# A token mixer's shift and scale from a four-column stationary operand, with a buffer for each weight tile, and other places for a gate chain and two gate sums

## The chip, the core and the metric

The kernel runs on one core of a Trainium2 chip. Its engines are TensorE (PE in the rows; PEld is its weight load), VectorE (DVE), ScalarE (ACT), GpSimd (POOL) and SyncE (SP), which issues the loads and stores. The metric is the time of one execution on the device in microseconds.

## What is computed

One layer of a bidirectional mLSTM mixer with a ConvGLU channel mixer, on 1024 latent tokens and 256 context tokens of width 1024. Each sub-layer is normalised and then shifted and scaled by a conditioning vector:

```python
mod = silu(c) @ w_mod + b_mod                      # w_mod (1024, 6 * 1024)
sh1, sc1, ga1, sh2, sc2, ga2 = split(mod, 6)
csh1, csc1, ... = split(silu(c_ctx) @ w_mod + b_mod, 6)
hc = rmsnorm(ctx, g_mix) * (1 + csc1) + csh1
hx = rmsnorm(x, g_mix) * (1 + sc1) + sh1
y  = mlstm_mixer(hx, hc, ...)                      # 4 heads, 2 directions, input and forget gates
x  = x + ga1 * y
hx = rmsnorm(x, g_ffn) * (1 + sc2) + sh2
gate, val = split(hx @ w_up, 2)                    # width 2816 each
x  = x + ga2 * ((silu(conv3(gate) + b_conv) * val) @ w_down)
return rmsnorm(x, g_final)
```

## The kernel before

Nearly all products are made from fp32 operands that `split` (L76) cuts in two: ScalarE casts a high part (`S.copy`), VectorE subtracts it for a low part, both in fp32r. `mm3` (L85) then makes three matmuls, high by high (L86), low by high (L87) and high by low (L88). The parts lie in eight buffers of the tag `w`. The writer's order is a wish: the framework places the instructions of each engine, and an engine runs its own in the order in which they then stand.

**The prelude.** `crow` holds `c` and `c_ctx`; after a transpose and a Silu they are `sct` (128 x 8 x 2: row block k, and the two vectors w), with the parts `sch` and `scl`. The loop at L211 goes over the eight row blocks k of `w_mod`, and in each over the two column blocks (shift, scale). It loads a tile `mr` of 128 x 1024 into one of six buffers and multiplies its two halves into four accumulators `mps` (2 rows by 512). For k = 1, 3, 5 the tile is split and goes through `mm3`; for the others it is multiplied in fp32 as it is (L227). Small loads stand between the tiles, and at k = 6 the context tokens are loaded and normalised (`x_load(0)`, `x_norm(0)`). Then come the first value weights `wv0` (loaded and split at L232), the latent tokens, and the way from accumulator to coefficient: `mrow` (copied out of PSUM), `mt` (sixteen transposes), `mts` (plus the bias), `smod` in `vec` (scale by gain). `x_trans` (L175) transposes the tokens and applies them (`xf`, L187), and the projections follow (`proj_v`, `pv`).

**The gate chain.** `gate_rows` (L393) makes from the gates' pre-activations `gt` all that the scans need: log-sigmoid, running sums and maxima along the tokens on VectorE, then `xc`, four columns of ends, transposed by TensorE as `cp`; a scan over the chunks in `gs`; `bp`, `mp` and `op` back through TensorE; `mx` is stored to `mdram`, and `cco`, `bco` are the coefficients. After it stands the projection of keys and queries of head 0, `proj_qk(0)`: `pk_256`, `pk_768`, `pk_0` (the context tokens, 24 matmuls of 256 columns) and `pq_256`, `pq_768`. The framework weaves the two.

**The channel mixer.** For each of 22 blocks ff of 128 channels TensorE makes seven products p1 to p7 (`products`, L907), twelve matmuls each, into eight PSUM accumulators of the tag `pp`; VectorE forms gate and value out of sums of them. Of steps 0 to 4, p1 and p2 are made ahead (`first`, L965; p1 is copied out as `e`), so that p2 stays in its accumulator until `gate0` (L971) has added it to `e`. `gate0` of steps 0 and 1 stands ahead of the loop (L1041), that of the others in the loop (L1066). `prep_rest` (L940) makes the operands of a step, `sa` and `sb`, and their splits `at` and `as`.

Of the kernel before, what the change touches and what calls it, by code (L numbers as in the profile page):

```python
# [39 lines left out]
def backbone(ctx, tc, x, c, ctxt, c_ctx, w_mod, b_mod, g_mix, g_ffn, w_in, b_gate,  # L40
# [170 lines left out]
    for k in range(KT):  # L211
        small_loads(k)
        if k == 6:
            x_load(0)
            x_norm(0)
        for w in range(2):
            r_ = mo.tile([P, D], F32, tag="mr", bufs=6, name=f"mr{k}_{w}")
            nc.sync.dma_start(out=r_, in_=w_mod[k * P:(k + 1) * P, w * D:(w + 1) * D])

            parts = split(r_, f"mm{k}_{w}") if k in (1, 3, 5) else None  # L220
            for hf in range(2):
                cs = slice(hf * 512, (hf + 1) * 512)
# [170 lines left out]
    def gate_rows():  # L393
# [868 lines left out]
```

## Time and profile before

| | us |
|---|---|
| median of 3 runs (lowest, highest) | 1210.47 (1210.46, 1212.51) |
| the profiled execution, its own time | 1211.26 |
| its span in the trace | 1209.5 |
| mean granted TensorE clock, as a share of the full one | 0.996 |

A row of a timeline gives start and length in microseconds from the span's start, engine, source line, operation, the tile written and the tiles read, and in brackets how long the engine stood idle before it and what ended that. A matmul's length holds its pipeline; the distance of two starts is what it occupies the engine. Tiles are named without their numbers.

### The profile page before, as it was taken

To read this page: it belongs to the slowest core of one execution; us is meant where nothing else is said; L and a number is where in the kernel's file an instruction comes from. 1 tells how busy PE (TensorE), PEld (TensorE's weight loads), DVE (VectorE), ACT (ScalarE), POOL (GpSimd) and SP (SyncE) were. 2 spreads that over 40 slices of the span, in tenths; PEclk is the share of its full clock that TensorE was granted. 3 is DMA by queue.
4 is the path that set the end of the run, shared out by engine and by line. 5 is a ranking of instruction groups with operands and counts; after the bars stand their busy time and mean duration, and the time that the engine had idled before them with its cause. 6 is when DMAs were issued, how large, how long until landed. Compare 5 with 4: busy or idle time off the path is not lost.

```text
span 1209.5 us, 16061 instructions
## 1 busy us (share of the span) xinstructions
PE 1182.0 (98%) x5811; PEld 976.2 (81%) x5811; DVE 884.9 (73%) x1564; ACT 509.1 (42%) x911; POOL 58.1 (5%) x198
## 2 busy tenths in 40 slices
PE   7999999999999999999999999999999999999996
PEld 1788998888888888887778888888888888888885
DVE  3775565576477568647999787778798877986887
ACT  3853353354255435236533333323333334445452
POOL 0100010011000001003000000000000000000011
PEclk9999999999999999999999999999999999999998
DMA  8622242343245441133233313244544569535523
GB/s 318 227 71 63 79 135 84 94 141 103 67 146 156 151 154 39 44 137 122 70 105 105 105 53 105 86 141 139 175 150 164 187 241 387 196 95 168 165 67 122
DMA packets 122289, 161.98 MB, mean 134 GB/s; under 512 B 8157, under 2 KB 84189, under 8 KB 122209
## 3 DMA queue, kind: packets, MB, share of 16 engines
q1 hardware_dynamic: 122208, 160.94, 40.1%
q8 instruction: 46, 0.75, 0.3%
q14 instruction: 35, 0.28, 0.1%
HBM read 126.27 MB, written 34.64 MB: 133 GB/s over the span
## 4 chain that ended last, share of the span: by engine, by line
PE 49%; DVE 3%; ACT 0%; issue 0%; POOL 0%; DMA 0%; DVEq 0%; POOLq 0%; ACTq 0%
PE p L86 11%; PE p L87 11%; PE p L88 11%; PE pa L87 3%; PE pa L88 3%; PE pa L86 3%; PE pb L87 2%; PE pb L88 2%; PE pb L86 2%; DVE bt L861 1%; DVE dr L1182 0%; DVE bs L878 0%; DMA rv<-in_f_w_up_dram 0%; DVE bu L861 0%; DVE sb L878 0%
## 5 line engine op out<-in xcount | busy, mean ns | idle before, releaser
L878 DVE TENSOR_TENSOR e<-e,p 128x512 f32<-128x512 f32 x66 | 45.0, 685 | 8.2 <-PE p L88 8.1
L983 ACT ACTIVATE t<-gt,cols 128x1024 f32<-128x1024 f32 x22 | 27.4, 1245 | 54.3 <-DVE gt L878 54.2
L989 ACT ACTIVATE t<-t 128x1024 f32<-128x1024 f32 x22 | 23.4, 1062 | 55.9 <-DVE t L986 55.9
L878 DVE TENSOR_TENSOR gt<-e,p 128x512 f32<-128x512 f32 x66 | 45.0, 684 | 2.1 <-PE p L88 1.9
L611 DVE SCALAR_TENSOR_TENSOR ha<-ha,hms,so 128x256 f32<-128x256 f32 x32 | 15.4, 481 | 41.5 <-POOL hms L126 41.5
L341 ACT CAST vh<-pv 128x256 fp32r<-128x256 f32 x30 | 11.1, 370 | 56.1 <-PE pv L88 56.1
L984 DVE SCALAR_TENSOR_TENSOR t<-gt,cols,t 128x960 f32<-128x960 f32 x22 | 26.8, 1216 | 10.7 <-ACT t L983 10.7
L88 PE MATMUL p<-bt,av 128*128 128x512 f32 x88 | 34.3, 389 | 0.0
L86 PE MATMUL p<-bt,av 128*128 128x512 f32 x88 | 34.2, 389 | 0.0
L87 PE MATMUL p<-bt,av 128*128 128x512 f32 x88 | 34.2, 389 | 0.0
L125 POOL TENSOR_SCALAR fms<-fms 128x1 f32<-128x1 f32 x8 | 3.8, 471 | 621.9 <-DVE fms L878 621.9
L342 DVE TENSOR_TENSOR vl<-pv,vh 128x256 fp32r<-128x256 f32 x30 | 12.6, 421 | 28.5 <-ACT vh L341 28.5
L86 PE MATMUL nm<-vh,wh 128*128 128x258 f32 x64 | 30.1, 471 | 0.0
L878 DVE TENSOR_TENSOR sa<-rv 128x512 f32<-128x512 f32 x22 | 15.2, 689 | 19.4 <-DMA rv<-in_f_w_up_dram 19.4
L604 ACT ACTIVATE ha<-nm,dn 128x256 f32<-128x256 f32 x32 | 15.1, 472 | 31.4 <-DVE dn L602 31.3
L577 ACT ACTIVATE wi<-mb,bco 128x128 f32<-128x128 f32 x64 | 22.6, 399 | 12.1 <-PE nm L594 7.9
L986 DVE SCALAR_TENSOR_TENSOR t<-gt,cols,t 128x960 f32<-128x960 f32 x22 | 26.7, 1214 | 0.0
L512 ACT ACTIVATE kh<-kt,cco 128x128 fp32r<-128x128 f32 x44 | 15.8, 367 | 23.8 <-PE kt L505 15.4
L86 PE MATMUL pk<-hx,wk_0h 128*128 128x512 f32 x64 | 25.3, 396 | 0.0
L86 PE MATMUL pq<-hx,wq_0h 128*128 128x512 f32 x64 | 25.2, 394 | 0.0
L88 PE MATMUL pq<-hx,wq_0h 128*128 128x512 f32 x64 | 25.2, 393 | 0.0
L87 PE MATMUL pk<-hx,wk_0l 128*128 128x512 f32 x64 | 25.0, 391 | 0.0
(1096 smaller groups left out, 4173.4 us busy)
## 6 DMA issues: line engine op xcount, KB each, us to landing
rg<-in_f_w_up_dram SPq DMA_DIRECT2D x26, 512.0 KB, 3.7
rv<-in_f_w_up_dram SPq DMA_DIRECT2D x22, 512.0 KB, 4.0
actd<-t SPq DMA_DIRECT2D x22, 512.0 KB, 3.1
dr<-in_f_w_down_dram SPq DMA_DIRECT2D x44, 256.0 KB, 5.2
dr<-sums SPq DMA_DIRECT2D x44, 256.0 KB, 2.8
dr<-actd SPq DMA_DIRECT2D x33, 256.0 KB, 5.1
mr<-in_w_mod_dram SPq DMA_DIRECT2D x16, 512.0 KB, 6.9
vor<-in_a_w_in_dram SPq DMA_DIRECT2D x24, 256.0 KB, 4.0
```

The costliest lines, as they stand in the source:

```text
L86: T.matmul(ps, ah, bh, start=first, stop=False)
L87: T.matmul(ps, al, bh, start=False, stop=False)
L88: T.matmul(ps, ah, bl, start=False, stop=last)
L512: S.mul(kh, tp[:, c0:c0 + P], wc)
L577: S.activation(out=wi[:, d, :], in_=mrow_, func=AF.Exp, scale=-1.0, bias=mpco[:, cc:cc + 1])
L604: S.mul(ha, nm[:, 0, :DV], dn[:, 0, :])
L611: V.scalar_tensor_tensor(out=ha, in0=ha, scalar=ms[:, 1:2], in1=so[i], op0=ALU.mult, op1=ALU.mult)
L878: V.tensor_tensor(out=out_, in0=a_, in1=b_, op=op)
L983: S.activation(out=t_, in_=gate, func=AF.Identity, scale=wcv[:, NFF + ff:NFF + ff + 1], bias=bcv[:, ff:ff + 1])
L984: V.scalar_tensor_tensor(out=t_[:, GRID_W:], in0=gate[:, :SEQ - GRID_W], scalar=wcv[:, ff:ff + 1], in1=t_[:, GRID_W:], op0=ALU.mult, op1=A ...
L986: V.scalar_tensor_tensor(out=t_[:, :SEQ - GRID_W], in0=gate[:, GRID_W:], scalar=wcv[:, 2 * NFF + ff:2 * NFF + ff + 1], in1=t_[:, :SEQ - GR ...
L989: S.activation(out=t_, in_=t_, func=AF.Silu)
```

## The change

In the prelude the stationary operand has four columns. `sc4` holds the high parts of the two vectors and beside them the low parts, so that one pass over a tile's high part and one over its low part give all four combinations; `sc0` holds the two vectors and two columns of zeros, for the tiles that are not split. The accumulators, `mrow` and `mt` are four wide, and the low columns are added to the high ones by one more sum into `mts`. All tiles but those of k = 0 and k = 7 are split. Each of the 16 tiles has a buffer of its own. The context tokens are loaded at k = 7, and their normalisation is written behind the loop.

`gate_rows` pauses in front of `cp`, five units of `proj_qk(0)` (all of the keys) are issued, and the `cp` transposes are placed behind the last TensorE instruction issued until then. And `gate0` of steps 2 and 3 is written ahead of the channel mixer's loop.

```diff
-    sch, scl = [mo.tile([P, KT, 2], F32R, name=n) for n in ("sch", "scl")]
-    V.tensor_copy(sch, sct)
-    V.tensor_tensor(out=scl, in0=sct, in1=sch.bitcast(F32), op=ALU.subtract)
+    sc4 = mo.tile([P, KT, 4], F32R, name="sc4")
+    V.tensor_copy(sc4[:, :, 0:2], sct)
+    V.tensor_tensor(out=sc4[:, :, 2:4], in0=sct, in1=sc4[:, :, 0:2].bitcast(F32), op=ALU.subtract)
+    sc0 = mo.tile([P, KT, 4], F32, name="sc0")
+    V.memset(sc0, 0.0)
+    V.tensor_copy(sc0[:, :, 0:2], sct)
...
-        if k == 6:
+        if k == KT - 1:
             x_load(0)
-            x_norm(0)
         for w in range(2):
-            r_ = mo.tile([P, D], F32, tag="mr", bufs=6, name=f"mr{k}_{w}")
+            r_ = mo.tile([P, D], F32, tag="mr", bufs=16, name=f"mr{k}_{w}")
             nc.sync.dma_start(out=r_, in_=w_mod[k * P:(k + 1) * P, w * D:(w + 1) * D])
-            parts = split(r_, f"mm{k}_{w}") if k in (1, 3, 5) else None
+            parts = split(r_, f"mm{k}_{w}") if 0 < k < KT - 1 else None
...
-                    mm3(p_, sch[:, k, :], scl[:, k, :], parts[0][:, cs], parts[1][:, cs], k == 0, k == KT - 1)
+                    for i in range(2):
+                        T.matmul(p_, sc4[:, k, :], parts[i][:, cs], start=False, stop=False)
                 else:
-                    T.matmul(p_, sct[:, k, :], r_[:, cs], start=k == 0, stop=k == KT - 1)
+                    T.matmul(p_, sc0[:, k, :], r_[:, cs], start=k == 0, stop=k == KT - 1)
+    x_norm(0)
...
-        T.transpose(mt[:, i * 2:i * 2 + 2], mrow[:, i // 4, (i % 4) * P:(i % 4 + 1) * P], ident[:2, :2])
+        T.transpose(mt[:, i * 4:i * 4 + 4], mrow[:, i // 4, (i % 4) * P:(i % 4 + 1) * P], ident[:4, :4])
...
+    V.tensor_tensor(out=mts, in0=mts, in1=mt4[:, :, 2:4], op=ALU.add)
...
+        yield
         cp = st("cp")
-        for i in range(2):
-            T.transpose(cp[:2, i * NR:(i + 1) * NR], xc[:, 2 * i:2 * i + 2], ident[:NR, :NR])
+        with behind(mybir.EngineType.PE):
+            for i in range(2):
+                T.transpose(cp[:2, i * NR:(i + 1) * NR], xc[:, 2 * i:2 * i + 2], ident[:NR, :NR])
...
-    gate_rows()
-    run(proj_qk(0))
+    rows_, qk0 = gate_rows(), proj_qk(0)
+    next(rows_)
+    for _ in range(5):
+        next(qk0)
+    run(rows_)
+    run(qk0)
...
+    gates += [gate0(ff, *pre[ff]) for ff in range(2, 4)]
...
-            if ff >= 2:
+            if ff >= 4:
                 gates.append(gate0(ff, e1, p2))
```

The order in which the built program's instructions stand moves at three places. The first is VectorE at the end of the prelude, from the copies out of PSUM to the split of the second half of the value weights. Before:

```order
L249 COPY mrow<-mw 2x512
L249 COPY mrow<-mp_117 2x512
L82 TENSOR_TENSOR wv00l<-wv0r_254,wv00h 128x1088
L254 TENSOR_TENSOR mts<-mt,bmc 128x32
L256 SCALAR_TENSOR_TENSOR vec<-mts,cols 128x16
L82 TENSOR_TENSOR wv01l<-wv0r_261,wv01h 128x1088
```

After:

```order
L255 COPY mrow<-mw 4x512
L255 COPY mrow<-mp_119 4x512
L261 TENSOR_TENSOR mts<-mt,bmc 128x32
L82 TENSOR_TENSOR wv00l<-wv0r_280,wv00h 128x1088
L262 TENSOR_TENSOR mts<-mts,mt 128x32
L263 SCALAR_TENSOR_TENSOR vec<-mts,cols 128x16
L82 TENSOR_TENSOR wv01l<-wv0r_287,wv01h 128x1088
```

The split `wv00l` stood ahead of the first instruction that reads the transposes `mt`, and stands now between the two sums that make `mts`, ahead of the scale in `vec`.

The second is the gate chain on TensorE, around `cp`. Before:

```order
L86 MATMUL pk_0_1108<-hxc_318,wk_0h 128x256
L87 MATMUL pk_0_1108<-hxc_318,wk_0l 128x256
L88 MATMUL pk_0_1108<-hxc_320,wk_0h 128x256
L439 MATMUL cp<-ident,gs_1005 2x40 x2
L86 MATMUL pk_0_1108<-hxc_318,wk_0h 128x256
L87 MATMUL pk_0_1108<-hxc_318,wk_0l 128x256
```

After:

```order
L86 MATMUL pk_0_1097<-hxc_346,wk_0h 128x256
L87 MATMUL pk_0_1097<-hxc_346,wk_0l 128x256
L88 MATMUL pk_0_1097<-hxc_348,wk_0h 128x256
L448 MATMUL cp<-ident,gs_1032 2x40 x2
L86 MATMUL pq_256_1167<-hx_357,wq_0h 128x512
L87 MATMUL pq_256_1167<-hx_357,wq_0l 128x512
```

`cp` stood behind the sixth of the 24 matmuls of `pk_0` and stands behind the last of them; the matmuls of `pq_256` follow, and `bp` comes behind fourteen of those (before, behind 16 more of `pk_0`). On VectorE, in the scan over the chunks behind `cp`, the split of the next head's key weights has come in. Before:

```order
L450 COPY gs_1004<-gs_1004 2x4x9
L451 TENSOR_TENSOR gs_1004<-gs_1004 2x40
L456 TENSOR_TENSOR gs_1005<-gs_1004,ident 2x80
L452 TENSOR_TENSOR gs_1004<-gs_1004 2x40
L456 TENSOR_TENSOR gs_1005<-gs_1004,ident 2x80
```

After:

```order
L459 COPY gs_1031<-gs_1031 2x4x9
L82 TENSOR_TENSOR wk_0l<-wk_r_1639,wk_0h 128x1024
L460 TENSOR_TENSOR gs_1031<-gs_1031 2x40
L465 TENSOR_TENSOR gs_1032<-gs_1031,ident 2x80
L461 TENSOR_TENSOR gs_1031<-gs_1031 2x40
L465 TENSOR_TENSOR gs_1032<-gs_1031,ident 2x80
```

The split `wk_0l` stood behind the whole chain, ahead of the copy into `cco`.

The third is VectorE ahead of step 0 of the channel mixer and in it; the digit behind a tile's letters is the step. Before:

```order
L861 TENSOR_TENSOR bt2_3_5730<-bs1_3_6130,bt2_3_5730 128x512
L878 TENSOR_TENSOR sa1_6464<-rv1_6462 128x512
L878 TENSOR_TENSOR sb1_6465<-rg1_6460,rv1_6462 128x512
L878 TENSOR_TENSOR sa1_6464<-sa1_6464,rg1_6460 128x512
L878 TENSOR_TENSOR sb1_6465<-rg1_6460,sa1_6464 128x512
L82 TENSOR_TENSOR at1l_6471<-sb1_6465,at1h_6470 128x1024
L878 TENSOR_TENSOR sa2_6578<-rv2_6576 128x512
L82 TENSOR_TENSOR as1l_6475<-sa1_6464,as1h_6474 128x1024
```

After:

```order
L874 TENSOR_TENSOR bt2_3_5757<-bs1_3_6157,bt2_3_5757 128x512
L891 TENSOR_TENSOR gt2_6422<-e2_6305,p2_2_6292 128x512
L891 TENSOR_TENSOR gt3_6424<-e3_6347,p2_3_6334 128x512
L891 TENSOR_TENSOR sa1_6495<-rv1_6493 128x512
L891 TENSOR_TENSOR sb1_6496<-rg1_6491,rv1_6493 128x512
L891 TENSOR_TENSOR sa1_6495<-sa1_6495,rg1_6491 128x512
L891 TENSOR_TENSOR sb1_6496<-rg1_6491,sa1_6495 128x512
L82 TENSOR_TENSOR at1l_6502<-sb1_6496,at1h_6501 128x1024
L82 TENSOR_TENSOR as1l_6506<-sa1_6495,as1h_6505 128x1024
L891 TENSOR_TENSOR sa2_6609<-rv2_6607 128x512
```

The two gate sums have come in ahead of `sa1`, and `as1l` stands ahead of `sa2`. The sum of `e0` and `p6` of step 0 comes six instructions behind `as1l` before, and seven behind it after.

## Rows read from the trace of the kernel before

**Rows 1.** The page, part 1: busy time of each engine, its share of the span and its instructions.

```profile
PE 1182.0 (98%) x5811; PEld 976.2 (81%) x5811; DVE 884.9 (73%) x1564; ACT 509.1 (42%) x911; POOL 58.1 (5%) x198
```

**Rows 2.** What TensorE (PE) waited for in the whole span: engine, line and what it waited for, then us in total, times, longest us. Three of the entries are shown.

```profile
PE p L86 <- DVE e L878: 2.9, 1, 2.9
PE mw L227 <- DMA mr<-in_w_mod_dram: 2.8, 1, 2.8
...
PE cp L439 <- DVE gs L434: 1.3, 1, 1.3
```

**Rows 3.** TensorE's timeline in the shift-and-scale products: start us, us, then engine, line, operation and operands; x4 is four records in a row. Shown are the two tiles of k = 2 (unsplit), the first and the last of ten split matmuls in a row, and the last four records.

```profile
14.08 1.88 PE L227 MATMUL mw<-mr,vec 128*2 128x512 f32 x4
...
15.79 1.88 PE L227 MATMUL mp<-mr,vec 128*2 128x512 f32 x4
...
18.07 0.40 PE L88 MATMUL mw<-mm_0l,sch 128*2 128x512 f32 x1
...
20.15 0.39 PE L88 MATMUL mp<-mm_1l,sch 128*2 128x512 f32 x1
...
33.00 1.88 PE L227 MATMUL mp<-mr,vec 128*2 128x512 f32 x4
```

**Rows 4.** Four stretches of 10 us from the start: bounds, length, busy us of PE, PEld, DVE, ACT and POOL, granted TensorE clock, mean share of the DMA engines, GB/s.

```profile
0.00:10.00 10.00, 4.42 (x8) 0.93 (x9) 2.69 (x9) 2.38 (x3) 1.78 (x28) 1.00 0.71 229
10.00:20.00 10.00, 9.82 (x33) 2.28 (x32) 4.90 (x4) 3.26 (x4) 0.00 (x0) 1.00 0.92 314
20.00:30.00 10.00, 9.54 (x31) 2.15 (x30) 3.98 (x6) 4.39 (x6) 0.90 (x2) 1.00 1.02 407
30.00:40.00 10.00, 9.34 (x51) 4.62 (x50) 5.94 (x14) 5.77 (x9) 0.00 (x0) 1.00 1.07 381
```

**Rows 5.** SyncE's queue: the issue of the seventh and eighth `w_mod` tile.

```profile
11.41 0.81 SPq L218 DMA_DIRECT2D mr<-in_w_mod_dram  x2
```

**Rows 6.** The splits and the end of the prelude on ScalarE and VectorE: start us, us, operation.

```profile
15.15 1.04 ACT L81 CAST mm_0h<-mr 128x1024 fp32r<-128x1024 f32 x1 [3.40 <-DMA mr<-in_w_mod_dram]
...
16.23 1.23 DVE L82 TENSOR_TENSOR mm_0l<-mr,mm_0h 128x1024 fp32r<-128x1024 f32 x1 [3.22 <-ACT mm_0h L81]
...
28.88 1.42 DVE L173 TENSOR_SCALAR xt<-xt,rs 128x1024 f32<-128x1024 f32 x2 [0.58 <-POOL rs L126]
...
35.67 1.29 DVE L82 TENSOR_TENSOR wv00l<-wv0r,wv00h 128x1088 fp32r<-128x1088 f32 x1
...
37.38 1.93 ACT L187 ACTIVATE xf<-tp,mts,vec 128x256 f32<-128x256 f32 x4 [0.74 <-DVE vec L256]
```

**Rows 7.** The gate chain: TensorE from the first `pk_0` matmul on the context tokens, and what stands beside it on VectorE and ScalarE, in order of start.

```profile
92.60 0.28 PE L86 MATMUL pk<-hxc,wk_0h 128*128 128x256 f32 x1
...
93.19 0.28 PE L88 MATMUL pk<-hxc,wk_0h 128*128 128x256 f32 x1
...
94.80 0.23 PE L439 MATMUL cp<-ident,gs 40*2 40x40 f32 x2 [1.33 <-DVE gs L434]
...
95.98 0.19 DVE L451 TENSOR_TENSOR gs<-gs 2x40 f32<-2x40 f32 x1
...
97.06 0.53 PE L459 MATMUL bp<-gs,ones 2*128 2x160 f32 x2
...
98.02 0.28 PE L88 MATMUL pk<-hxc,wk_0h 128*128 128x256 f32 x1
...
98.22 1.06 ACT L81 CAST wk_0h<-wk_r 128x1024 fp32r<-128x1024 f32 x1 [1.53 <-PE pk L87]
...
99.31 1.23 DVE L82 TENSOR_TENSOR wk_0l<-wk_r,wk_0h 128x1024 fp32r<-128x1024 f32 x1
```

**Rows 8.** TensorE around the first product of channel-mixer step 1: the first and the last matmul of `p6` of step 0, the first of step 1, and the first at the full pace after it.

```profile
603.61 0.39 PE L86 MATMUL p<-bt,as0h 128*128 128x512 f32 x1
...
606.11 0.39 PE L88 MATMUL p<-bt,as0h 128*128 128x512 f32 x1
...
609.44 0.76 PE L86 MATMUL p<-bt,as1h 128*128 128x512 f32 x1 [2.94 <-DVE e L878]
...
612.87 0.39 PE L88 MATMUL p<-bt,as1h 128*128 128x512 f32 x1
```

**Rows 9.** VectorE ahead of and in step 0 of the channel mixer: a split and the sums after it, `sa` of steps 1 and 2, the sum on `p6` of step 0, `sa` of step 3.

```profile
579.54 1.22 DVE L82 TENSOR_TENSOR ag3l<-rg,ag3h 128x1024 fp32r<-128x1024 f32 x1
580.68 3.09 DVE L878 TENSOR_TENSOR bs<-bs,bs 128x512 f32<-128x512 f32 x5
...
596.25 0.69 DVE L878 TENSOR_TENSOR sa<-rv 128x512 f32<-128x512 f32 x1
...
602.67 0.69 DVE L878 TENSOR_TENSOR sa<-rv 128x512 f32<-128x512 f32 x1 [1.40 <-DMA rv<-in_f_w_up_dram]
...
608.61 0.68 DVE L878 TENSOR_TENSOR e<-e,p 128x512 f32<-128x512 f32 x1
...
610.17 0.69 DVE L878 TENSOR_TENSOR sa<-rv 128x512 f32<-128x512 f32 x1 [0.88 <-DMA rv<-in_f_w_up_dram]
```

**Rows 10.** Three stretches with the columns of rows 4: that of the gate chain, and two after TensorE's wait in the channel mixer.

```profile
90.00:100.00 10.00, 8.67 (x53) 7.14 (x51) 8.44 (x32) 3.89 (x7) 0.00 (x0) 1.00 0.01 4
...
608.00:610.00 2.00, 0.56 (x1) 0.50 (x2) 1.29 (x2) 0.39 (x1) 0.00 (x0) 0.83 1.06 313
610.00:612.00 2.00, 2.00 (x6) 1.61 (x5) 1.62 (x3) 0.00 (x0) 0.00 (x0) 0.50 0.58 173
```

More of the change, by code (lines that the diff above doesn't have):

```diff
@@ L212, in backbone @@
         small_loads(k)
-        if k == 6:
+        if k == KT - 1:
             x_load(0)
-            x_norm(0)
         for w in range(2):
-            r_ = mo.tile([P, D], F32, tag="mr", bufs=6, name=f"mr{k}_{w}")
+            r_ = mo.tile([P, D], F32, tag="mr", bufs=16, name=f"mr{k}_{w}")
             nc.sync.dma_start(out=r_, in_=w_mod[k * P:(k + 1) * P, w * D:(w + 1) * D])
-            parts = split(r_, f"mm{k}_{w}") if k in (1, 3, 5) else None
+            parts = split(r_, f"mm{k}_{w}") if 0 < k < KT - 1 else None
             for hf in range(2):
                 cs = slice(hf * 512, (hf + 1) * 512)
-                p_ = mps[w * 2 + hf][:2, :]
+                p_ = mps[w * 2 + hf][:4, :]
                 if parts:
-                    mm3(p_, sch[:, k, :], scl[:, k, :], parts[0][:, cs], parts[1][:, cs], k == 0, k == KT - 1)
-                else:
-                    T.matmul(p_, sct[:, k, :], r_[:, cs], start=k == 0, stop=k == KT - 1)
+                    for i in range(2):
+                        T.matmul(p_, sc4[:, k, :], parts[i][:, cs], start=False, stop=False)
+                else:
+                    T.matmul(p_, sc0[:, k, :], r_[:, cs], start=k == 0, stop=k == KT - 1)
+    x_norm(0)
     VG = DV + 16
@@ L245, in backbone @@
     V.tensor_copy(bmc, pc[:, P:P + 48])
-    mrow = mo.tile([2, 4, 512], F32, name="mrow")
+    mrow = mo.tile([4, 4, 512], F32, name="mrow")
     for i in range(4):
-        (V.tensor_copy if i % 2 else S.copy)(mrow[:, i, :], mps[i][:2, :])
+        (V.tensor_copy if i % 2 else S.copy)(mrow[:, i, :], mps[i][:4, :])
     mt = st("mt")
     for i in range(16):
-        T.transpose(mt[:, i * 2:i * 2 + 2], mrow[:, i // 4, (i % 4) * P:(i % 4 + 1) * P], ident[:2, :2])
+        T.transpose(mt[:, i * 4:i * 4 + 4], mrow[:, i // 4, (i % 4) * P:(i % 4 + 1) * P], ident[:4, :4])
     mts = const.tile([P, 16, 2], F32, name="mts")
-    V.tensor_tensor(out=mts, in0=mt[:, 0:32].rearrange("p (i w) -> p i w", w=2),
-                    in1=bmc[:, 0:16].unsqueeze(2).to_broadcast([P, 16, 2]), op=ALU.add)
+    mt4 = mt[:, 0:64].rearrange("p (i w) -> p i w", w=4)
+    V.tensor_tensor(out=mts, in0=mt4[:, :, 0:2], in1=bmc[:, 0:16].unsqueeze(2).to_broadcast([P, 16, 2]), op=ALU.add)
+    V.tensor_tensor(out=mts, in0=mts, in1=mt4[:, :, 2:4], op=ALU.add)
     V.scalar_tensor_tensor(out=smod, in0=mts[:, 8:16, :], scalar=1.0,
```

## The prediction

> **What bounds the kernel now.** I read the busy times first [rows 1]: TensorE is busy 1182.0 of 1209.5 us, VectorE 884.9, ScalarE 509.1. So the end is set by TensorE, and an edit pays only where TensorE stands still, or does work that it need not do. Then I read the list of what TensorE waited for [rows 2]. It has three entries of over a microsecond beside the lines that change: 2.8 us for the first weight tile (the same tile comes first afterwards), 2.9 us on a sum of the first channel-mixer step, and 1.3 us in front of the `cp` transposes. The third thing to see is no wait: until 34.9 us TensorE is occupied with the shift-and-scale products [rows 3], while the loads behind them are let out in pieces [rows 5] and the DMA engines reach 407 GB/s only after 20 us [rows 4].
>
> **The shift and scale: work.** An unsplit weight tile costs TensorE 1.71 us (from one tile's first record to the next tile's, 14.08 to 15.79 [rows 3]). A split tile's matmuls stand (20.15 - 18.07) / 9 = 0.231 us apart [rows 3]; six of them are 1.39 us, the four of the new form 0.92. Before: 10 x 1.71 + 6 x 1.39 = 25.4 us. After: 4 x 1.71 + 12 x 0.92 = 17.9. That is 7.5 us less on TensorE. Two more stationary columns cost nothing in this count, because a record's length goes with the 512 moving columns (0.40 with two columns as well). ScalarE and VectorE get six more splits, 1.04 and 1.23 us each [rows 6]. They hide as long as a tile takes no less to arrive: 0.524 MB at 407 GB/s is 1.29 us. The three small operations that make the two stationary operands hide behind the first load, which TensorE awaits for 2.8 us [rows 2].
>
> **The shift and scale: what is late next.** With a buffer for each tile nothing holds back the loads (before, the seventh went out at 11.41 us [rows 5]). Up to the last `w_mod` tile stand 16 tiles and two context tiles, 18 x 0.524 + 0.09 = 9.53 MB. By 10 us 2.29 MB had come, by 30 us 2.29 + 3.14 + 4.07 = 9.50 [rows 4]. So before the last tile was there at about 30 us and TensorE ended at 33.00 + 1.88 = 34.88: TensorE was late. After, at the rate of 20 to 30 us, the last tile comes at 10 + 7.24 / 0.407 = 27.8 us; the tile before it at 26.5. Two unsplit tiles from 26.7 on end at 30.3. With 381 GB/s (30 to 40 us) the tile comes at 29.0 and the end is 31.1; with 314 (10 to 20 us) at 33.1 and 35.2. I take 30.5, since the 314 hold the waits for buffers. From the last product to the first `xf` it was 37.38 - 34.88 = 2.50 us [rows 6]. That grows: the split `wv00l` (1.29 us, 35.67) was done while VectorE waited for the transposes, and now stands between the first and the new second sum of `mts`, in front of `smod`. Its pitch of 1.20 and the added sum of 0.2 make 1.4 us. So `xf` starts at 30.5 + 2.5 + 1.4 = 34.4 and not at 37.38: **3.0 us gained**, between 3.1 (the fastest rate) and a loss of 1.7 (314 GB/s). What follows keeps its order on all engines up to the gate chain, and the first latent tile, two tiles behind `wv0`, comes at about 32, before its use, so I let the whole of it through. `x_norm(0)` now stands behind twelve splits: its tile is there at 25, its two squares and scalings (1.42 us, 28.88 [rows 6]) fit before 30.
>
> A page speaks against this. The trace shows 407 GB/s over ten microseconds [rows 4]. The Trainium skill, "DMA: Bandwidth & Descriptors", section "Bandwidth", lets the HBM side bind such loads at about 358 GB/s a core; by that the last tile would come at 30.2, the products would end at 32.3, and 1.2 us of the 3.0 would stay. The trace disagrees with it here, and the sum goes by the rows.
>
> **The gate chain.** TensorE's sixth `pk_0` matmul starts at 93.19, pitch 0.12, and `cp` at 94.80 after a wait of 1.33 [rows 7]: 1.49 us are lost to the scan's last copy. Now `cp` stands behind all 24 of them, at 92.60 + 24 x 0.118 = 95.44, when its operand is ready (94.8). What may be late next is `bp`. Before, `cp` to the sum of L451 took 1.18 us and from there to `bp` 1.08 [rows 7]. Now the split `wk_0l` of the next head stands between the chain's copy and that sum. It needs a cast that starts 0.2 us after the last `pk_0` matmul (98.02, 98.22 [rows 7]), so at 95.5; the split then runs from 96.6 (99.31 before), and the next sum starts 1.14 later, at 97.75. `bp` can go at 98.83. TensorE reaches it after `cp` and fourteen `pq` matmuls, at a pitch of 0.23 as in [rows 3, 8]: 95.60 + 14 x 0.23 = 98.8. So nothing is lost there. The `mb` rows follow the chain, which ends some 1.8 us later than before; they stand on ScalarE in front of `qT` and the first `kh`, which by the same counting are ready about when TensorE wants them. I take **1.3 us gained**, between 1.5 and nothing: no row shows the new order, and the nearest is the 1.33 itself.
>
> **The two gate sums.** At 606.34 TensorE has eight full accumulators: five products of step 0 and the second product of steps 2, 3 and 4, whose gate sum had not been taken. It waits until VectorE gets to the sum on `p6` at 608.61 [rows 9], and goes on at 609.44 [rows 8], at first slowly: the granted clock is 0.83 from 608 to 610 and 0.50 from 610 to 612 [rows 10], which is the lower of its two levels, 1.2 GHz, and what came before the fall was these 2.94 us of standing. The matmul at 612.87 is the first at the full pace. At the pace of 0.227 ([rows 8], 603.61 to 606.11) it would start at 606.11 + 9 x 0.227 = 608.15: **4.7 us**. With the sums of steps 2 and 3 taken before, two accumulators are free and `p6`, `p5` of step 1 need no sum of step 0. I count VectorE through, with pitches of 0.60 for a sum and 1.14 for a split [rows 9]. The two sums move `sa` from 596.25 to 597.45. The split `as1l` now follows `at1l` and ends at 603.6, wanted at 606.57. `sa` of step 2 waits for its tile (602.67 before, with the load let out 1.2 later: 603.9), so the sum on `p6` starts at about 608.8 as before. But it is wanted only by the third product, at 606.34 + 2 x 2.72 = 611.8. Behind it `sa` of step 3 waits for its tile until about 610.4 (610.17 before [rows 9]), and then 23 sums and 7 longer ones end with `as3l` at 610.4 + 13.8 + 8.0 + 0.6 = 632.8, wanted at 606.34 + 10 x 2.72 + 0.23 = 633.8. That is the tightest place. VectorE's two sums before the loop cost it 1.2 us in a stretch where TensorE has its operands for 3 us ahead; the loop has 1.2 us less. Ends: 4.7 gained, or nothing if a stall of that kind comes back further on. I take 4.7.
>
> **Sum.** 3.0 + 1.3 + 4.7 = 9.0. The profiled execution took 1211.26 us (its span 1209.5), the median of the runs is 1210.47. 1211.3 - 9.0 = 1202.3 by the one, 1201.5 by the other; I predict 1202.0.
>
> **Rivals.** (a) The stall in the channel mixer only moves: the sums that free accumulators stand behind `sa` of step 3, which waits for a load. If that load lands after 612.7 and not at 610.4, or `as3l` slips by over 1 us, TensorE stands again. For it speaks VectorE's load, against it margins of 2 to 3 us everywhere else. It gives back about 3 of 4.7: 1205. (b) The prelude yields nothing, because the loads run at a rate nearer to 350 and `wv00l` comes late: 1205. (c) TensorE's clock falls after the wait for the last two tiles. Then their eight records cost 0.43 more each, 3.4 us, and the 32 transposes some 0.6: 1206. For it speaks that TensorE now works 0.92 us in 1.29 for each tile; against it that the stand of 1.33 us in front of `cp` left the granted clock of its stretch at 1.00 [rows 7, 10]. (d) On the other side: the lower clock holds from 10.7 us on through the whole prelude. Twelve split tiles at 1.85 us end at 32.9, two unsplit ones at 3.42 at 39.7, 9.2 later than forecast, and the transposes add 2.0: 1202.0 + 11.2 = 1213.2, slower by 2.7. It decides once slow work costs more than 8.5 us. Against it: the granted clock reads 1.00 in every stretch of the prelude [rows 4], with gaps of 0.5 us between tiles. That the edits don't take place is no rival: the order of the built program shows each of them.
>
> A rule bears on (c) and (d): the Trainium skill, "TensorE: Matmul & The Clock Gate", section "HAM oscillation — how this bites in real kernels", tells of loops whose matmuls on a tile are shorter than the wait for the next tile and which fall back to the lower clock at each tile. By that rule the time would be that of (d); the trace has its one fall after a stand of 2.94 us [rows 8, 10], and no row shows shorter ones doing it.
>
> **How the numbers follow.** Forecast 0.66 (its own range 1200.0 to 1204.0: 407 or 381 GB/s, and the gate chain's ends), (a) 0.12, (b) 0.08, (c) 0.10, (d) 0.04. The range 1200.0 to 1206.0 takes in the forecast, (a), (b) and half of (c). About 0.2%, 2.4 us, is what a measurement of this kernel can tell from no change. All cases but (d) are faster by more than that; I keep 0.04 for bad ends of (a) to (c) that meet: faster 0.92, same 0.04, slower 0.04.
>
> **What would show it.** Right: the first `xf` near 34.4, the last product near 30.5, full DMA rate from 10 us on; `cp` without a wait and `bp` with at most 0.2; no wait at the first product of step 1, granted clock 1.00 from 600 to 620, and no new wait up to step 4. Wrong: `xf` not before 36; waits at `bp` or `dc`; a TensorE wait between 610 and 640; a granted clock below 1.00 before 40 us.

## The result, and the profile after

| | before | after |
|---|---|---|
| median of 6 runs each, us (lowest, highest) | 1211.49 (1209.69, 1213.64) | 1203.48 (1202.40, 1204.71) |
| span of the profiled execution, us | 1209.5 | 1202.4 |
| that execution's own time, us | 1211.26 | 1204.13 |

The ratio is 0.9934, with a 95% interval of 0.9921 to 0.9947: 8.0 us faster by the medians (6.4 to 9.6 by the interval), where 9.0 were forecast. The page's busy times, against [rows 1]; TensorE (PE) is busy for 6.2 us less:

```profile
PE 1175.8 (98%) x5799; PEld 974.8 (81%) x5799; DVE 891.1 (74%) x1573; ACT 514.5 (43%) x917; POOL 58.0 (5%) x198
```

The list of what TensorE waited for, against [rows 2]: the two entries that the change was to remove are gone, and four new ones stand there (the wait for `xf` is not new: it was 1.4 before).

```profile
PE mw L231 <- DMA mr<-in_w_mod_dram: 3.3, 2, 2.6
PE pr L148 <- DMA crow<-in_c_ctx_dram: 2.7, 1, 2.7
...
PE tp L186 <- ACT xf L191: 1.3, 2, 0.7
PE tp L186 <- DVE mts L262: 1.3, 1, 1.3
...
PE mp L229 <- DVE mm_1l L82: 1.0, 3, 0.5
PE p L87 <- DVE as19l L82: 0.9, 1, 0.9
...
PE p L87 <- DVE as17l L82: 0.6, 1, 0.6
```

The waits for `mm_1l`, of 0.5 us at most, lie between the split tiles, where TensorE has time until the next tile lands; the other three are followed below.

Where the time came from is best read off the same matmul in both traces. The lead over the trace of before (a matmul's start in before minus its start in the other trace, in us, median of 25 neighbouring matmuls; one trace a row) at six places, for the changed kernel and the experiments below:

| trace | first products on `hx` (48.3 in before) | behind the gate chain (104.3) | end of the mixer (540) | step 2 of the channel mixer (613.8) | behind step 19 (950) | last matmuls (1199.5) |
|---|---|---|---|---|---|---|
| after | 2.24 | 3.69 | 3.75 | 8.51 | 6.93 | 7.13 |
| e10, the same kernel again | 1.49 | 2.91 | 2.93 | 7.71 | 8.25 | 8.52 |
| e1, prelude alone | 1.84 | 1.91 | 1.81 | 2.89 | 3.43 | 3.74 |
| e2, gate chain alone | -0.04 | 1.35 | 1.35 | 1.29 | 1.62 | 1.91 |
| e3, gate sums alone | 0.36 | 0.35 | 0.24 | 5.04 | 5.58 | 5.61 |
| e4, `as` split first | 1.99 | 3.38 | 3.36 | 8.14 | 8.68 | 8.97 |
| e9, `wv00l` behind `smod` | 2.96 | 4.39 | 4.42 | 9.18 | 9.71 | 9.98 |

In the row of after: prelude 2.24 (forecast 3.0), gate chain 1.45 (1.3), gate sums 4.76 (4.7), then a loss of 1.58 that was not in the sum. The 0.54 that most of the others gain between step 2 and step 19 (0.33 in e2) is what before itself lost there.

**The prelude.** First the windows of after (against [rows 4]), the columns as there: PEclk, DMA share and GB/s stand last.

```profile
10.00:20.00 10.00, 9.35 (x33) 2.40 (x32) 9.09 (x10) 7.78 (x9) 0.00 (x0) 1.00 1.03 407
20.00:30.00 10.00, 8.35 (x28) 1.82 (x27) 7.49 (x8) 6.89 (x9) 0.90 (x2) 1.00 1.05 400
30.00:40.00 10.00, 8.09 (x56) 6.65 (x54) 7.90 (x22) 8.00 (x14) 0.00 (x0) 0.83 1.05 406
34.00:36.00 2.00, 0.88 (x5) 0.67 (x6) 1.97 (x6) 1.32 (x3) 0.00 (x0) 0.76 1.03 420
36.00:38.00 2.00, 2.00 (x10) 2.00 (x10) 1.96 (x8) 2.00 (x6) 0.00 (x0) 0.50 1.02 420
38.00:40.00 2.00, 2.00 (x16) 2.00 (x16) 1.83 (x7) 2.00 (x5) 0.00 (x0) 0.89 1.03 404
```

The full DMA rate stands from 10 us on, as forecast. TensorE's granted clock stays at 1.00 through the twelve split tiles, and falls to 0.50 (1.2 GHz) behind them. What the engine did before shows in its timeline, and in those of VectorE and ScalarE:

```profile
27.27 1.88 PE L231 MATMUL mw<-mr,sc 128*4 128x512 f32 x4 [0.71 <-DMA mr<-in_w_mod_dram]
28.98 1.88 PE L231 MATMUL mp<-mr,sc 128*4 128x512 f32 x4
...
34.52 0.63 PE L186 MATMUL tp<-ident,xt 128*128 128x128 f32 x4 [1.31 <-DVE mts L262]
35.75 1.11 PE L186 MATMUL tp<-ident,xt 128*128 128x128 f32 x4 [0.60 <-ACT xf L191]
36.52 0.80 PE L86 MATMUL pv<-wv00h,hxc 128*128 128x272 f32 x2
```

```profile
32.88 0.19 DVE L261 TENSOR_TENSOR mts<-mt,bmc 128x32 f32<-128x32 f32 x1 [1.30 <-PE mt L258]
32.99 1.29 DVE L82 TENSOR_TENSOR wv00l<-wv0r,wv00h 128x1088 fp32r<-128x1088 f32 x1
34.19 0.18 DVE L262 TENSOR_TENSOR mts<-mts,mt 128x32 f32<-128x32 f32 x1
...
34.68 1.93 ACT L191 ACTIVATE xf<-tp,mts,vec 128x256 f32<-128x256 f32 x4 [1.56 <-DVE vec L263]
```

The last product ends at 28.98 + 1.88 = 30.86 (forecast 30.5) and the first `xf` starts at 34.68 (34.4): 2.70 earlier than the 37.38 of [rows 6], and so 0.3 short of the forecast 3.0. `wv00l` stands between the two sums, as forecast; that TensorE stands for the second sum, because the third group of transposes needs the buffer of `mt` (`st`, three buffers), which that sum is the last to read, was not in the forecast.

**The gate chain**, against [rows 7]: `cp` follows the last matmul of `pk_0` without a wait, and `bp` follows fourteen matmuls of `pq`.

```profile
93.03 0.28 PE L88 MATMUL pk<-hxc,wk_0h 128*128 128x256 f32 x1
93.25 0.23 PE L448 MATMUL cp<-ident,gs 40*2 40x40 f32 x2
93.41 0.50 PE L86 MATMUL pq<-hx,wq_0h 128*128 128x512 f32 x1
...
96.48 0.39 PE L87 MATMUL pq<-hx,wq_0l 128*128 128x512 f32 x1
96.80 0.53 PE L468 MATMUL bp<-gs,ones 2*128 2x160 f32 x2
```

**Step 1 of the channel mixer**, against [rows 8, 10]: the first product of step 1 (`as1h`) starts one pitch of 0.23 behind the last one of step 0, and the clock is full where it was 0.83 and 0.50.

```profile
602.36 0.39 PE L88 MATMUL p<-bt,as0h 128*128 128x512 f32 x1
602.59 0.39 PE L86 MATMUL p<-bt,as1h 128*128 128x512 f32 x1
```

```profile
606.00:608.00 2.00, 2.00 (x10) 1.68 (x9) 1.40 (x3) 0.00 (x0) 0.00 (x0) 1.00 0.80 240
608.00:610.00 2.00, 2.00 (x10) 1.66 (x9) 2.00 (x4) 0.82 (x1) 0.00 (x0) 1.00 0.00 0
```

**Steps 17 and 19.** VectorE's and TensorE's timelines of after around the two new waits (the last two rows are the second):

```profile
885.20 0.69 DVE L891 TENSOR_TENSOR sa<-rv 128x512 f32<-128x512 f32 x1 [0.98 <-DMA rv<-in_f_w_up_dram]
885.93 0.69 DVE L891 TENSOR_TENSOR sa<-sa,rg 128x512 f32<-128x512 f32 x1
...
890.60 1.22 DVE L82 TENSOR_TENSOR as17l<-sa,as17h 128x1024 fp32r<-128x1024 f32 x1
...
890.91 0.39 PE L86 MATMUL p<-bt,as17h 128*128 128x512 f32 x1
891.87 0.50 PE L87 MATMUL p<-bt,as17l 128*128 128x512 f32 x1 [0.57 <-DVE as17l L82]
...
924.53 0.69 DVE L891 TENSOR_TENSOR sa<-rv 128x512 f32<-128x512 f32 x1 [1.13 <-DMA rv<-in_f_w_up_dram]
...
931.20 0.50 PE L87 MATMUL p<-bt,as19l 128*128 128x512 f32 x1 [0.95 <-DVE as19l L82]
```

The same place in the trace of before, where the split ends just as TensorE comes to it:

```profile
893.18 0.69 DVE L878 TENSOR_TENSOR sa<-rv 128x512 f32<-128x512 f32 x1 [1.18 <-DMA rv<-in_f_w_up_dram]
...
898.57 1.22 DVE L82 TENSOR_TENSOR as17l<-sa,as17h 128x1024 fp32r<-128x1024 f32 x1
...
899.84 0.50 PE L87 MATMUL p<-bt,as17l 128*128 128x512 f32 x1
```

`as17l` needs nothing of the `sa` at 885.20, which is the next step's. It stands behind it and the six operations after it in VectorE's order, and `sa` stands for its load. From the start of `sa` to that of `as17l` it is 5.4 us, here and in before (893.18 to 898.57). So the time of `as17l` is set by when that load lands.

### The profile page after: what moved, and what is told of

Its sections match the earlier page's. It is cut to its first block, busy times and chain, and to the rows that moved or that the text cites. A ratio compares the mean times of both kernels' runs of the same rounds, so it can differ in the third digit from the quotient of the medians.

```text
span 1202.4 us, 16048 instructions
## 1 busy us (share of the span) xinstructions
PE 1175.8 (98%) x5799; PEld 974.8 (81%) x5799; DVE 891.1 (74%) x1573; ACT 514.5 (43%) x917; POOL 58.0 (5%) x198
## 4 chain that ended last, share of the span: by engine, by line
PE 43%; DVE 6%; DMA 2%; issue 1%; POOL 0%; ACT 0%; DVEq 0%; POOLq 0%; ACTq 0%; SPq 0%
PE p L87 9%; PE p L88 9%; PE p L86 9%; PE pa L87 3%; PE pa L86 3%; PE pa L88 3%; PE pb L88 2%; PE pb L87 2%; PE pb L86 2%; DMA rv<-in_f_w_up_dram 2%; DVE e L891 1%; DVE t L997 0%; DVE sr L891 0%; DVE gt L891 0%; DVE t L999 0%
## 5 line engine op out<-in xcount | busy, mean ns | idle before, releaser
L997 DVE SCALAR_TENSOR_TENSOR t<-gt,cols,t 128x960 f32<-128x960 f32 x22 | 26.7, 1215 | 10.6 <-ACT t L996 10.6
L87 PE MATMUL pq<-hx,wq_0l 128*128 128x512 f32 x64 | 25.1, 392 | 0.0
```

Source lines behind the costliest of these rows:

```text
L87: T.matmul(ps, al, bh, start=False, stop=False)
L997: V.scalar_tensor_tensor(out=t_[:, GRID_W:], in0=gate[:, :SEQ - GRID_W], scalar=wcv[:, ff:ff + 1], in1=t_[:, GRID_W:], op0=ALU.mult, op1=A ...
```

## The experiments

Each part of the change alone, on the kernel before (the diff is that part of the change's diff). One session; before took 1211.05 in it.

**e1, the prelude alone.**

> The kernel before with the shift and scale alone changed. In the changed kernel's trace the first xf comes 2.70 us earlier and TensorE's products behind it 2.24 us earlier (46.09 against 48.33), because its clock falls after the wait of 1.31 us in front of the x transposes. Theory (the three parts add up, each by its own stage): 2.2 us gained, 1209.3 if the kernel before takes 1211.5; granted clock near 0.5 around 37 us. Rival (part of the 2.2 comes from the gate chain's new order, which the prelude's loads reach): under 1.5 us gained. Waits at as17l and as19l: none if they belong to the gate sums, between 0 and 1.5 us if they hang on when the rv loads land.

1208.14 us, ratio 0.9981 (0.9972 to 0.9990). The lead is 1.84 behind the prelude and stays; the clock reads 0.64 from 36 to 38 and 0.51 from 38 to 40. So the prelude's gain is its own, a bit smaller here than in after. The stall at step 1 cost 1.1 us less here than in the trace of before (1.81 to 2.89), in a place that this part does not touch: TensorE stands there for 2.77 us where it was 2.94, and the granted clock stays at 1.00 from 606 to 614 where it fell to 0.50. No wait at `as17l`.

**e2, the gate chain alone.**

> The kernel before with the gate chain's new place alone. Theory: cp without a wait behind 24 matmuls of pk_0, bp without a wait, 1.5 us gained: 1210.0 if the kernel before takes 1211.5, which the timing can barely tell from no change; the trace should show TensorE's matmuls from 101 us on 1.5 us earlier. Rival (the new order only works with the earlier loads of the new prelude): a wait at bp or at mb, gain under 0.7 us.

1209.62 us, ratio 0.9991 (0.9982 to 1.0000). 1.39 us appear between 48 and 104 (-0.04 to 1.35) and stay. `cp` starts at 95.58, 0.21 behind the last `pk_0` matmul at 95.37, without a wait. The theory holds without the new prelude.

**e3, the gate sums alone.**

> The kernel before with the two gate sums alone moved. Theory: no wait at the first product of step 1, clock 1.00 from 600 to 620, 4.7 us gained up to step 2, and behind it between 0 and 1.5 us lost at as17l and as19l, by when the rv loads land: 1206.8 to 1208.3 if the kernel before takes 1211.5. Rival one (the new waits at as17l and as19l come from the two moved sums, since VectorE's queue is another from there on): the full 1.5 us lost here and nothing of it without this part. Rival two (the stall needs the earlier prelude too): under 3 us gained.

1206.04 us, ratio 0.9963 (0.9951 to 0.9976). 4.80 us appear between 540 and 613.8 (0.24 to 5.04), and there is no wait at `as17l` or `as19l`. Both rivals fall in this trace: the moved sums alone bring no waits, and their gain does not need the new prelude. The three parts alone add up to 2.9 + 1.4 + 5.0 = 9.3 us.

**e4, the `as` split first**, on the changed kernel:

```diff
-        h_, l_ = split(sb, f"at{ff}")
-        aw[ff, 7], aw[ff, 3] = ...
-        yield
-        h_, l_ = split(sa, f"as{ff}")
-        aw[ff, 5], aw[ff, 6] = ...
-        yield
+        for n, s_, i, j in (("at", sb, 7, 3), ("as", sa, 5, 6))[::-1 if ff else 1]:
+            h_, l_ = split(s_, f"{n}{ff}")
+            aw[ff, i], aw[ff, j] = ...
+            yield
```

> The changed kernel with the split of sa (as..) traced ahead of the split of sb (at..) from step 1 on, so that VectorE has as17l and as19l before it stands at the next step's sa, which waits for its load. Theory (TensorE's new waits of 0.6 and 0.9 us are VectorE standing behind a load with as..l in its queue): both waits are gone, the at splits are in time since their products come two products later (5.4 us), and 1.5 us are gained on the changed kernel's profiled span: about 1201 of 1202.4. Rival (VectorE's own work per step is the bound in steps 13 to 20): a wait of the same size at at..l or at a gate sum, time unchanged.

1202.58 us, ratio 0.9933 (0.9921 to 0.9946). VectorE's timeline:

```profile
878.55 1.21 DVE L82 TENSOR_TENSOR as17l<-sa,as17h 128x1024 fp32r<-128x1024 f32 x1
882.70 0.69 DVE L891 TENSOR_TENSOR sa<-rv 128x512 f32<-128x512 f32 x1 [1.42 <-DMA rv<-in_f_w_up_dram]
888.10 1.22 DVE L82 TENSOR_TENSOR at17l<-sb,at17h 128x1024 fp32r<-128x1024 f32 x1
```

`as17l` is done over 11 us before TensorE wants it (891.50), `at17l` has taken its place and is in time. No wait is left, and the lead from 613.8 to 950 grows by 0.54 where it fell by 1.58. With the new order the split no longer hangs on the next step's load; that no wait is left shows less by itself, since e10 below has none with the old order either. The time says less still: its span is 1200.5, 1.9 under that of after, but 2.16 us lie outside it (1.73 in after; why stays open).

**e5, the splits of `wv0` behind `smod`**, on the changed kernel (e5 to e8 stand beside 1210.42 us for before; `last` is the instruction of `smod`):

```diff
-        wv0.append(split(r_, f"wv0{kh}"))
+        wv0.append(r_)
...
     hmod = mts[:, 0:8, :]
+    with tc.issue_after(last):
+        wv0 = [split(r_, f"wv0{kh}") for kh, r_ in enumerate(wv0)]
```

> The changed kernel with the splits of wv0 traced behind smod and queued behind it on VectorE, so that the two sums of mts and smod follow each other at once. In the changed kernel TensorE waits 1.31 us for the second sum, starts the x transposes at 34.52, and its granted clock is 0.76 from 34 to 36 us and 0.50 from 36 to 38. Theory (wv00l between the sums is what makes TensorE stand, and the stand is what makes the clock fall): first xf at about 33.5 where it was 34.7, TensorE's wait in front of the transposes under 0.3 us, clock 1.00 throughout, its products behind the prelude 1.2 + 0.8 = 2.0 us earlier than in the changed kernel. Rival one (the clock falls for the thin work ahead, 8.35 us busy of 10 from 20 to 30, whatever stands at 33): the clock still falls, about 1.2 us gained. Rival two (wv00l and wv01l are then late for the first products): TensorE waits there, under 0.5 us gained.

1202.11 us, ratio 0.9931 (0.9915 to 0.9948). TensorE's wait for `mts` is 0.2, the clock stays at 1.00 throughout, and the first `pv` product comes 1.06 us earlier than in after (35.46 against 36.52). Of that 0.17 is left at the first product on `hx`: `wv01h` now stands between the `xf` on ScalarE, and TensorE waits for `hxc` and for the next tokens instead. (The same kernel as after, traced again as e10, has 1.49 at that place and not 2.24, so 0.17 is well inside what one trace can vary by.) Rival one falls, and the theory is right on the clock and wrong on the gain; the edit moved too much to tell what the clock costs, which e9 does.

**e6, 16 buffers and nothing else**, on the kernel before:

```diff
-            r_ = mo.tile([P, D], F32, tag="mr", bufs=6, name=f"mr{k}_{w}")
+            r_ = mo.tile([P, D], F32, tag="mr", bufs=16, name=f"mr{k}_{w}")
```

> The kernel before with 16 buffers for the weight tiles and nothing else. Theory (TensorE's 25.4 us of shift and scale products set the end of the prelude, not the loads): DMA near 407 GB/s from 10 us on, the last tile some 3 us before TensorE comes to it, first xf within 0.5 us of 37.4, time unchanged. Rival (the loads held back by buffers set the end, the fewer matmuls only follow): first xf near 35, 2 us gained.

1209.80 us, ratio 0.9994 (0.9985 to 1.0003): no change that can be measured. The DMA moves 398 GB/s from 10 to 20 us instead of 314, and the first `xf` comes at 36.64, 0.74 earlier, a little more than I gave it. Earlier loads alone are worth little while TensorE has 25 us to do.

**e7, six buffers again**, on the changed kernel: the same line the other way round.

> The changed kernel with 6 buffers for the weight tiles again, the 4-column products kept. Theory (with TensorE's work down to 17.9 us the loads set the end, and they need the buffers): a buffer goes round in 6.8 us of load and some 2.5 us of splits, so a tile comes every 1.55 us where it was 1.29, the last one about 2.6 us later; the first xf near 37, most of the prelude's gain gone, 2 us slower than the changed kernel. Rival (six buffers are enough for the new form): first xf within 0.5 us of 34.7.

1204.90 us, ratio 0.9956 (0.9941 to 0.9971). TensorE comes to the last two tiles at 29.84 after a wait for the load, 2.57 later than in after, and the DMA is back at 329 GB/s:

```profile
10.00:20.00 10.00, 7.70 (x27) 1.61 (x25) 7.17 (x6) 6.17 (x6) 0.00 (x0) 1.00 0.94 329
```

The first `xf` starts at 37.24 and the lead behind the prelude is 0.15. So neither half of the prelude's edit gains much by itself (0.15 here, 0.75 by the trace of e6): fewer matmuls without the buffers wait for loads, and buffers without fewer matmuls wait for TensorE.

**e8, one gate sum moved and not two**, on the changed kernel:

```diff
-    gates += [gate0(ff, *pre[ff]) for ff in range(2, 4)]
+    gates += [gate0(ff, *pre[ff]) for ff in range(2, 3)]
...
-            if ff >= 4:
+            if ff >= 3:
```

> The changed kernel with the gate sum of step 2 alone moved in front of the loop, that of step 3 back in its step. Theory (TensorE waited for a free accumulator of eight, and each moved sum frees one): the first product of step 1 starts without a wait, the second, wanted 2.72 us later, waits for VectorE's sum on p6 until about 1 us after that, under 1.5 us lost in all, clock 1.00. Rival (it is VectorE's queue that got shorter in the loop, not the accumulators): the wait comes back by half at the first product of step 1, over 2 us lost.

One run, 1203.61 us. No wait at either product, clock 1.00, 4.79 us between 540 and 613.8 (2.36 to 7.15): the whole gain. The second product starts at 607.35, and VectorE's sum had started at 605.64:

```profile
605.64 0.68 DVE L891 TENSOR_TENSOR e<-e,p 128x512 f32<-128x512 f32 x1
```

The rival falls; my own wait of 1 us came from taking that sum's time from before (608.61), though the whole stretch comes earlier here. In this one trace a single free accumulator is enough; the second moved sum was not needed.

**e9, `wv00l` alone behind `smod`**: as e5, and the first `xf` held behind `wv01h` on ScalarE, by which all other engines keep the order of after.

```diff
+                with tc.issue_after(wv01h) if gi + k == 0 else ExitStack():
-                S.activation(out=t_, in_=tp[:, kk * 256:(kk + 1) * 256], func=AF.Identity,
-                             scale=smod[:, k, w:w + 1], bias=hmod[:, k, w:w + 1])
+                    S.activation(out=t_, in_=tp[:, kk * 256:(kk + 1) * 256], func=AF.Identity,
+                                 scale=smod[:, k, w:w + 1], bias=hmod[:, k, w:w + 1])
```

> The changed kernel with one thing moved: on VectorE the split wv00l stands behind smod and no longer between the two sums of mts; every other engine keeps its order. Before this, with both splits of wv0 late, the clock stayed at 1.00, but TensorE's products behind the prelude gained 0.17 us only. Theory (the prelude after its last product is a chain on ScalarE and VectorE, xf, squares and casts, and TensorE's stand and clock inside it are cover): first xf at 33.5 and no stand of over 0.3 us in front of the transposes, but the first pv product still near 36.5, since wv00l and wv01l stand in front of the first cast; under 0.8 us gained behind the prelude. Rival (TensorE's stand and its lower clock are the price): 1.5 to 2 us gained behind the prelude.

1202.95 us, ratio 0.9930 (0.9914 to 0.9945). Its windows, and TensorE's and VectorE's timelines:

```profile
34.00:36.00 2.00, 0.89 (x7) 0.42 (x4) 2.00 (x2) 2.00 (x5) 0.00 (x0) 1.00 1.03 424
36.00:38.00 2.00, 1.64 (x11) 1.42 (x12) 2.00 (x9) 1.75 (x4) 0.00 (x0) 1.00 1.02 414
```

```profile
33.60 0.63 PE L186 MATMUL tp<-ident,xt 128*128 128x128 f32 x4 [0.23 <-DVE mts L263]
34.83 0.66 PE L186 MATMUL tp<-ident,xt 128*128 128x128 f32 x4 [0.60 <-ACT xf L192]
36.35 0.52 PE L86 MATMUL pv<-wv00h,hxc 128*128 128x272 f32 x2 [0.86 <-DVE hxc L194]
...
33.59 1.29 DVE L82 TENSOR_TENSOR wv00l<-wv0r,wv00h 128x1088 fp32r<-128x1088 f32 x1
34.81 1.28 DVE L82 TENSOR_TENSOR wv01l<-wv0r,wv01h 128x1088 fp32r<-128x1088 f32 x1
36.01 0.49 DVE L194 CAST hxc<-xf 128x256 fp32r<-128x256 f32 x2
```

The stand of 1.31 is 0.23 and the clock does not fall. The first `pv` product is no earlier (36.35 against 36.52), since the two splits still stand in front of the first cast; but its successors run at the full pace, and the lead behind the prelude is 2.96. That is 0.72 more than in after, within the theory's bound of 0.8, but 1.47 more than in e10, the kernel without this edit traced beside it, which is just short of the rival's 1.5. In e10 the first `pv` product comes at 36.37, so that all of the 1.47 arises behind it, at the lower clock: the clock is not mere cover, as the theory had it.

**e10, the changed kernel again; e11, e4 and e9 together; e12, e11 with `wv01l` behind the first two pairs of casts as well.** Before took 1211.63 us beside e9 to e12. The edit of e12 beyond e11, in `x_trans(0)`:

```diff
+            if k2 == 1 and gi == 0:
+                with queued(mybir.EngineType.DVE):
+                    V.tensor_tensor(out=wv1[1], in0=wv1_raw, in1=wv1[0].bitcast(F32), op=ALU.subtract)
```

> The changed kernel once more, beside the two last versions. Theory (the new waits at as17l and as19l hang on when the rv loads land, not on the change): other landing times and so other waits there, 0 to 1.5 us in sum, while the prelude, the gate chain and step 1 repeat to 0.3 us. Rival (the waits are part of the new program): 0.6 and 0.9 us again.

1202.41 us, ratio 0.9921 (0.9907 to 0.9934). No wait at `as17l` or `as19l` (lead 7.71 to 8.25). Its timeline of VectorE: `sa` has its load 2.2 us earlier than in after, and the split follows by the same 5.4.

```profile
882.98 0.69 DVE L891 TENSOR_TENSOR sa<-rv 128x512 f32<-128x512 f32 x1 [1.22 <-DMA rv<-in_f_w_up_dram]
888.37 1.22 DVE L82 TENSOR_TENSOR as17l<-sa,as17h 128x1024 fp32r<-128x1024 f32 x1
```

The same program has the waits in one trace and not in the other: they hang on the landing of the loads. The prelude did not repeat to 0.3: the stand of 1.31 is there again, the clock falls later (0.78 from 36 to 38, 0.50 from 38 to 40) and the lead is 1.49.

> The changed kernel with the splits of sa ahead of those of sb and wv00l behind smod. Theory: the 0.9 us of the first and what the second gave alone, add up: 1201.5 to 1202.5, no wait at as..l. Rival (nothing left to gain beside the noise of the loads): the same as the changed kernel run beside it, within 0.5 us.

1202.88 us, ratio 0.9925 (0.9912 to 0.9937). By the trace both parts are there (lead 2.99 behind the prelude, no wait at `as..l`, 10.01 at the end, span 1199.5). By the times it can't be told from the changed kernel beside it: the rival holds.

> As the version with sa first, and with wv00l behind smod and wv01l behind the first two pairs of casts, so that the first products of pv have their operands about 1.2 us earlier. Theory (VectorE's two splits ahead of the first cast set the first pv product): it starts near 35.3 where it was 36.5, and 0.5 to 1 us more is gained than with wv00l moved alone: 1201 to 1202. Rival (the next row of x tiles sets what follows, through its squares on ScalarE): first pv earlier, but the first product on hx no earlier, under 0.3 us gained.

1204.16 us, ratio 0.9938 (0.9925 to 0.9950). The first `pv` comes at 34.81, 1.71 earlier than in after, and then the framework places the later transposes and splits in another order: TensorE waits 1.4 us for a `gt`, its clock reads 0.50 from 50 to 52, and the lead behind the gate chain is 2.22 where e11 has 4.41. No version here measurably beats the changed kernel.

## Why the prediction was right, point by point

**What TensorE waited for.** The prediction reads three entries of over a microsecond beside the lines that change. The whole list of before has three more: 2.8 us for `crow`, 2.0 for `xn` and 1.4 for `xf`. After the change they are 2.7, 2.0 and 1.3, so that the sum does not suffer by it.

**The prelude: work and loads, right.** 407 GB/s from 10 us on, the last two tiles at 27.27 (forecast 26.7), the last product's end at 30.86 (30.5), the first `xf` at 34.68 (34.4). e6 and e7 show both halves of the argument: TensorE was late before, and the loads are late after. The Trainium skill's "DMA: Bandwidth & Descriptors", section "Bandwidth", was quoted against it (about 358 GB/s from the HBM side); the same section gives that figure for two cores that stream at once, and up to 425 for one core alone. The trace, of one core, has 407, 400 and 406 over three stretches of 10 us.

**The prelude: what is late next, the step that was mis-sized.** I let the 3.0 us of `xf` through in whole, and 2.24 came (1.84 and 1.49 in e1 and e10). Of the 0.76 that lack in after, 0.3 lie ahead of `xf`, which came 2.70 earlier, and 0.46 behind it. I had `wv00l` in front of the second sum, and its 1.4 us, but not that TensorE stands for that sum and that its clock may fall behind it. That is rival (c) at another place: not the last two tiles (their stand was 0.71 and their clock 1.00) but the transposes and first `pv` products ran at 1.2 GHz. The sign was among those named for being wrong, a granted clock below 1.00 before 40 us, and it came; its price was not rival (c)'s 4.0 us. From the first `xf` to the first product on `hx` 0.46 and 0.53 us are lost in after and e4, where the clock falls before 36 us, and 0.95 to 1.0 in e1, e8 and e10, where it falls behind 36 and so on `pv` products alone. In e7, with the same stand and no fall, nothing is lost (0.14 and 0.15): by that trace the price is the clock's and not the stand's. e9 takes the stand away and moves nothing else, the clock stays, and the lead is 2.96 (2.99 in e11, with the same order). That this meets the 3.0 of the sum is in part luck, since `xf` starts 3.62 earlier there, at 33.76, and 0.66 of it is not let through.

**The gate chain, right.** 1.45 in after, 1.42 in e10, 1.39 alone in e2, for 1.3. `bp` was reached 0.32 behind the last matmul in front of it, a pitch and 0.1.

**The gate sums, right.** 4.76 in after and 4.78 in e10, 4.80 alone in e3, for 4.7; the clock is 1.00 from 600 to 620. VectorE's count came out too: `as3l` ends at 628.01 + 1.22 = 629.2; the forecast 632.8 less the lead of 3.75 is 629.05. That two sums had to move was more than needed (e8).

**Rival (a), in a place that I did not look at.** I gave the channel mixer margins of 2 to 3 us everywhere but at `as3l`. At `as17l` and `as19l` the trace of before had none: its `as17l` ended at 898.57 + 1.22 = 899.79, TensorE took it at 899.84, and by the leads of the others it lost 0.54 us over both. In after 2.1 us were lost there (1.58 and those 0.54). The waits are not in e3, nor in e10, which is the same program as after, so the change does not bring them every time; that `as17l` stands behind a load is the order on VectorE, which e4 changes. The waits are why the profiled execution of after shows 7.1 and not 8.5 to 9 us.

**Rivals (b) and (d) fell.** The loads were not slower than the rows of before let expect, and the clock was 1.00 through the split tiles, so that the slower case had nothing to rest on. Nor did (d) follow from the rule set beside it, the Trainium skill's "TensorE: Matmul & The Clock Gate", section "HAM oscillation — how this bites in real kernels": that is told of matmuls shorter than the wait for the next tile, and here they take 0.92 of 1.29 us, the longer part. In the trace the clock was 1.00 there.

**The sum.** 2.24 + 1.45 + 4.76 - 1.58, and 0.26 at the ends, is 7.13 in the trace of after, and 8.52 in that of e10; by the medians it is 8.0 and 9.2, for 9.0. Where between these a run falls is the luck of the loads at steps 17 and 19 and of the clock in the prelude, neither of which the sum held.

## What to carry to other kernels

An edit that lets an engine through sooner should be followed to the next thing that the engine stands for, not only to the next result: here the second sum was priced for `xf`, and the lower clock behind TensorE's stand for it took 0.5 to 1.0 us of the 3.0. Look for operations whose operands are long ready and that stand in an in-order queue behind one that waits for a load: their lateness is the load's, changes from run to run, and goes with a change of order. And where two limits lie close together (TensorE's work and the loads), half an edit gains little, so each half tried alone says nothing against the whole.

## What was not expected of the hardware

**The clock behind a stand.** Six traces have the stand of 1.31 us in front of the transposes with 0.60 behind it (after, e1, e4, e7, e8, e10). In five of them the granted clock falls to 0.50 afterwards, in two between 34 and 36 us (0.76 in after, 0.84 in e4) and in three between 36 and 38 (0.64 in e1, 0.72 in e8, 0.78 in e10); in e7 it stays at 1.00 with the same stand. The traces without the stand (before, e2, e3, e5, e6, e9, e11, e12) have no fall there; e12 has one later, to 0.50 from 50 to 52, behind waits of 0.58, 0.85 and 1.37 between 45 and 48.7. So the stand is what goes before the fall, and is not enough for it; what tells e7 apart stays open. The stand of 1.33 in front of `cp` [rows 7] left the clock alone. At step 1 of the channel mixer the stands of 2.94 and 2.97 us in before and e2 were followed by 0.50, while those of 2.77 in e1 and in e6 left it at 1.00; whether their length or something else decides stays open.

**The loads' landing.** The `rv` load of step 17, issued with the same work around it, took 6.21 us in before, 6.27 in after, 4.44 in e1 and 4.79 in e10 from its issue (867.97, 860.13, 864.64 and 859.14) to the sum that reads it. The load of step 18, behind which `as17l` stands, took 3.9 to 4.2 in all four, and was issued 14.86 us after that sum in each: the profile has the last sum into `sb` of step 17 release it (in after that sum ends at 881.23 and the issue is at 881.26). So a late load is handed on to the next through VectorE's order, and what differs at `as17l` had arisen at least one load earlier. In e1 `as17l` was done 2.3 us before TensorE wanted it; in before and after it was late. Why the first of the two loads takes 4.4 us here and 6.3 there stays open.
